# Small parameter loads moved to GpSimd's queue, eight unread products, and two changes of order in an attention and mLSTM trunk

## The chip, the cores and the metric

One core of a Trainium2 chip runs the whole program. The metric is device microseconds of one execution, from a batch of runs that gives a median. A profiled execution of the same program gives the spans, waits and clocks below.

## What is computed

A trunk of two layers over 256 tokens of width 1024, batch 1, in float32. Layer 0 mixes tokens by native sparse attention (16 heads in 4 groups, a compressed, a selected and a sliding branch), layer 1 by a chunkwise mLSTM. Each layer is modulated by a conditioning vector c:

```
shift, scale, gate = split(c @ ada_w[i] + ada_b[i], 3)
h = rmsnorm(x, norm_g[i]) * (1 + scale) + shift
y = nsa_mixer(h, ...) if i == 0 else mlstm_mixer(h, ...)
x = x + gate * y
...
return rmsnorm(x, final_g)
```

In the attention, `k_cmp` and `v_cmp` come from a small two-layer network over blocks of tokens (weights `a_cmp_w1`, `a_cmp_w2`, biases `a_cmp_b1`, `a_cmp_b2`, positions `a_cmp_pe`). The mLSTM has a short convolution on q and k (`b_conv_w`, `b_conv_b`) and a gain per column (`b_head_g`).

## The kernel before, in words

Weights stream from HBM as float32 into a ring of ten raw tiles. Each is split in two fp32r halves, high (`wh`, ScalarE, L165) and low (`wl`, VectorE, L170), and a float32 product is made of three fp32r products on TensorE. The order of the work in layer 0 is written out by hand: inside `manual_schedule` (L387) the instructions of TensorE, ScalarE, VectorE and SyncE stand as the program lists them. GpSimd is not in that list, so a scheduler places its instructions.

**First phase** (`first_phase`, L392, some 60 us). The input projection runs over eight blocks of 128 rows of the weight. For block kk the products are `proj` (L470 to L480): 42 of 128x256 at L480, in three groups of wh, wl and the low half of the activations. Before a block can start, its 128 columns of shift and scale must be known. They come from 1 MB of `ada_w` for each block (tiles `Q`, `KH`, `KL`, multiplied by c on ScalarE at L423 and VectorE at L425 into `adaA`), and `columns` (L427) sums them over partitions by eight products with a single column (L432), after which VectorE adds biases (L434, L435) and ScalarE makes the block's activations (L439). `columns` for block kk + 1 stands after product 30 of block kk, and for the first block after its last product, so that TensorE has nothing to do until L439 is done.

**SyncE's queue** issues every big load, in the order of use (`_load_one`, L72 to L92). Of one block these are 512 KB and 384 KB of `a_w_in` and four of 256 KB of `ada_w`. The fourteen small parameter loads of `small_loads` (L325; 428 KB together) stand in a list, and from the thirteenth big load on one of them follows each big load (L89, L90):

```
for dst, src in pieces:
    self.nc.sync.dma_start(dst(v), src)
if self.small and self.loaded >= self.SMALL:
    self.nc.sync.dma_start(*self.small.pop(0))
```

Five fill `pra` (positions, gains and biases of layer 0 and 1), three fill `prb` (the mLSTM's convolution and gains), and six are the compression network's biases and second weights (`b1bc`, `b2v`, `w2k`, `w2v`). `parameters` (L460), in the seventh block, turns `pra` and `prb` by two TensorE transpositions into columns.

**Attention** (`nsa`, L581). Eight more blocks project the remaining keys and values (`kv_block`), then the compression network (`hidden`, L606, two halves around the scores `S(0)`), then the scores `S(n)`, the exponentials `softmax(n)` (ScalarE, L988), their scaling `scaled(n, j)` (VectorE, L1005), transpositions `T_pair` (L1018) and values `PV` (L1039), for n from 0 to 7, with parts of the z path and of the gates between them. `z_out` (L918) reads the PSUM bank of the z path, and `gate_steps` (L922) takes the same bank over with 16 products at L227. `dup_split` (L559) copies keys between partitions on GpSimd (L571), once at the end of the first phase and once before `S(0)`. GpSimd otherwise makes masks and zeroes tiles.

Of the kernel before, what the change touches and what calls it, by code (L numbers as in the profile page):

```python
# [12 lines left out]
OP = mybir.AluOpType  # L13
AX = mybir.AxisListType

P = 128
# [7 lines left out]
class Kernel:  # L24
# [14 lines left out]


    RAW = 10
    SMALL = 12
    WBUF = 6

    def stream_init(self):
# [26 lines left out]
    def _load_one(self):  # L72
        kind, shape, pieces = self.queue[self.loaded]
        n = int(np.prod(shape[1:]))
        if self.loaded in self.homes:
            tag, part, bufs = self.homes[self.loaded]
            if not part:
                self.guests[tag] = self.T(self.p1, [P, 2048] if bufs == 1 else [P, 1024], tag=tag, bufs=bufs)
            raw = self.guests[tag][:, 1024 * part :]
        else:  # L80
            raw = self.pw.tile([P, 1024], F32, name=self.nm("raw"), tag="raw", bufs=self.RAW)
        v = raw[:, :n]
        if len(shape) == 3:
            v = v.rearrange("p (a b) -> p a b", a=shape[1])
        elif len(shape) == 4:
            v = v.rearrange("p (a b c) -> p a b c", a=shape[1], b=shape[2])
        for dst, src in pieces:
            self.nc.sync.dma_start(dst(v), src)  # L88
        if self.small and self.loaded >= self.SMALL:  # L89
            self.nc.sync.dma_start(*self.small.pop(0))  # L90
        self.raws[self.loaded] = v
        self.loaded += 1  # L92

# [231 lines left out]
    def small_loads(self):  # L325
        nc, t = self.nc, self.t
        row = lambda ap: ap.rearrange("(a p) -> a p", p=P)
        self.small = []
        self.small.append((self.pra[0:32], t["a_cmp_pe"][0].rearrange("j (u r) d -> (j u) (r d)", r=2)))
        self.small.append((self.pra[32:40], row(t["norm_g"][1])))  # L330
        self.small.append((self.pra[40:56], row(t["ada_b"][1, 0:2048])))
        for j in range(2):
            self.small.append((self.pra[56:57, 64 * j : 64 * j + 64], t["a_cmp_b2"][0, 0:1]))
        self.small.append((self.prb[0:64], t["b_conv_w"][0].rearrange("j (c p) -> (j c) p", p=P)))
        self.small.append((self.prb[64:80], row(t["b_conv_b"][0])))
        self.small.append((self.prb[80:96], row(t["b_head_g"][0])))
        for j in range(2):
            self.small.append((self.b1bc[64 * j : 64 * j + 64], t["a_cmp_b1"][0, j].partition_broadcast(64)))
        self.small.append((self.b2v, t["a_cmp_b2"][0, 1].partition_broadcast(P)))
        for j in range(2):  # L340
            self.small.append((self.w2k[:, :, j], t["a_cmp_w2"][0, 0].rearrange("(a p) d -> p a d", p=P)))
        self.small.append((self.w2v, t["a_cmp_w2"][0, 1].rearrange("(a p) d -> p a d", p=P)))


    def layer1(self):
        nc, t, pc, p1 = self.nc, self.t, self.pc, self.p1
        ident = self.ident
# [36 lines left out]
        self.stream_rest()  # L384
        self.small_loads()

        with self.tc.manual_schedule(engines={mybir.EngineType.PE, mybir.EngineType.Activation, mybir.EngineType.DVE, mybir.EngineType.SP}):  # L387
            self.first_phase(place)
            self.nsa(self.acc)
            self.boundary()  # L390

    def first_phase(self, place):  # L392
# [3 lines left out]
        bt = self.bank(6)  # L396
# [30 lines left out]
        def columns(kk, A):  # L427

            bank = self.bank(7)
            for b in range(2):  # L430
                for h in range(2):
                    nc.tensor.matmul(bank[:, b : b + 1], A[:, h, b * P : b * P + P], self.ones1, start=(h == 0), stop=(h == 1), skip_group_check=True)  # L432
            cols = self.T(pc, [P, 2], tag="cols", bufs=4)
            nc.vector.tensor_tensor(cols, bank[:, 0:2], pca[:, 16 + kk : 25 + kk : 8], op=OP.add)  # L434
            nc.vector.tensor_tensor(cols[:, 1:2], cols[:, 1:2], pca[:, 8 + kk : 9 + kk], op=OP.mult)  # L435
            return cols

# [22 lines left out]
        def parameters():  # L460
            bt = self.bank(7)
            nc.tensor.transpose(bt[:, 0:57], self.pra, ident[:57, :57])
            nc.tensor.transpose(bt[:, 64:160], self.prb, ident[:96, :96])
            nc.vector.tensor_copy(pca[:, 32:89], bt[:, 0:57])
            nc.vector.tensor_scalar(pca[:, 80:88], pca[:, 80:88], 1.0, None, op0=OP.add)
            pcb = self.pcb = self.T(pc, [P, 96])
            nc.vector.tensor_copy(pcb[:, 0:80], bt[:, 64:144])
            nc.vector.tensor_scalar(pcb[:, 80:96], bt[:, 144:160], 0.5, None, op0=OP.mult)

        def proj(kk):  # L470

# [34 lines left out]
        for kk in range(KC):  # L506

            if not kk:
                self.make_lo(*wide)
            if kk < KC - 1:  # L510
                A = self.T(pc, [P, 512], tag="adaA", bufs=2).rearrange("p (h m) -> p h m", h=2)
                rows(A, 0)
            if kk:
                h32 = self.T(p1, [P, SEQ], tag="y32", bufs=2)
                modulate(kk, h32, cols)
                rest(kk, h32)
            if kk < KC - 1:
                rows(A, 1)
            if kk:
                self.make(place[kk][1])  # L520
            if kk < KC - 1:
                parts = self.make_hi(place[kk + 1][0])
            else:
                self.mpos = max(place[kk]) + 1
                self.split_next()
            for n, _ in enumerate(proj(kk)):
                if (kk, n) == (6, 34):
                    parameters()
                if kk < KC - 1 and n == (29 if kk else 41):
                    cols = columns(kk + 1, A)  # L530
                    modulate(kk + 1, self.hh[:, kk + 1], cols)
                    self.make_lo(*parts)
                elif (kk, n) == (KC - 1, 17):
                    self.KH, self.KL = [self.T(p1, [P, 4, 512], F32R, tag=tag) for tag in ("KH", "KL")]
                    self.dup_split((self.KH, self.KL), 0, acc[6])
                    self.E, self.F = [], {}
                    self.evac_cmp(acc[4])
                    self.split_next()
                    self.evac_cmp(acc[5])
# [41 lines left out]
    def nsa(self, acc):  # L581
# [62 lines left out]
        self.S(0)  # L644
        self.softmax(0)
        hidden(2)
        hidden(3)

        h1 = self.T(p1, [P, 256], tag="y32", bufs=2)
# [105 lines left out]
        for a in range(2):  # L755
            nc.gpsimd.memset(Pc[a], 0.0)
            nc.vector.tensor_tensor(Pc[a][:, :, 0:16], Tc[:, a], mn[:, 16 * a : 16 * a + 16].unsqueeze(2).to_broadcast([P, 16, 16]), op=OP.mult)
        self.go(z, 8)
        self.S(3)
        self.scaled(2, 0)  # L760
        PcT = self.PcT = self.T(p1, [P, 4, SEQ])

        def cmp_transposed(i2):
# [4 lines left out]
            nc.scalar.activation(PcT[:, 2 * i2 : 2 * i2 + 2].rearrange("p i k -> p (i k)"), b, AF.Copy)  # L768

        cmp_transposed(0)  # L770
        self.softmax(3, (0,))
        self.scaled(2, 1)
        self.z_tanh(1)
        self.z_out(1)
        self.PV(1)
        self.gated(0, 0)

# [937 lines left out]
```

## Time and profile before

| What | us |
|---|---|
| median of 3 runs (459.8 to 460.69) | 460.62 |
| the profiled execution | 459.5 |
| its span, first to last instruction | 457.7 |
| TensorE busy in the span | 441.4 |
| VectorE, ScalarE, GpSimd busy | 340.7, 278.0, 37.9 |

The profiled execution is 1.1 us under the median. The page cuts the span in 40 slices of 11.4 us; digits are tenths of busy time, and PEclk is TensorE's granted clock in tenths of full speed. The chain of waits runs back from the last instruction to what released each step. An "x8" behind a row says that eight instructions are merged in it, so the start of the next row tells the pace.

### The profile page before, as it was taken

To read this page: it belongs to the slowest core of one execution; us is meant where nothing else is said; L and a number is where in the kernel's file an instruction comes from. 1 tells how busy PE (TensorE), PEld (TensorE's weight loads), DVE (VectorE), ACT (ScalarE), POOL (GpSimd) and SP (SyncE) were. 2 spreads that over 40 slices of the span, in tenths; PEclk is the share of its full clock that TensorE was granted. 3 is DMA by queue.
4 is the path that set the end of the run, shared out by engine and by line. 5 is a ranking of instruction groups with operands and counts; after the bars stand their busy time and mean duration, and the time that the engine had idled before them with its cause. 6 is when DMAs were issued, how large, how long until landed. Compare 5 with 4: busy or idle time off the path is not lost.

```text
span 457.7 us, 8171 instructions
## 1 busy us (share of the span) xinstructions
PE 441.4 (96%) x2938; PEld 378.5 (83%) x2938; DVE 340.7 (74%) x792; ACT 278.0 (61%) x549; POOL 37.9 (8%) x102
## 2 busy tenths in 40 slices
PE   7899899999999999999999999999999999999993
PEld 3899899889948777788899889988888888888882
DVE  3878768778959767587998369688986978545645
ACT  4746678466688588366956685655655555454614
POOL 8840020300000000012000000000000000000000
PEclk9989999999999999999999999999999999999997
DMA  8999996793377999899999999897845799740002
GB/s 271 337 313 297 338 373 188 200 364 91 95 208 253 275 236 307 254 194 164 215 172 115 95 291 314 155 170 232 261 127 204 203 230 243 245 139 0 1 0 93
DMA packets 74637, 94.58 MB, mean 207 GB/s; under 512 B 4652, under 2 KB 52068, under 8 KB 74596
## 3 DMA queue, kind: packets, MB, share of 16 engines
q1 hardware_dynamic: 74020, 92.73, 76.2%
q10 hardware_dynamic: 336, 0.80, 0.5%
q8 instruction: 23, 0.38, 0.3%
q0 software_dynamic: 240, 0.53, 0.3%
q14 instruction: 18, 0.15, 0.1%
HBM read 93.00 MB, written 1.05 MB: 205 GB/s over the span
## 4 chain that ended last, share of the span: by engine, by line
PE 82%; DMA 6%; DVE 5%; ACT 3%; SPq 2%; issue 1%; ACTq 0%
PE bank L579 9%; PE bank L577 9%; PE bank L578 9%; PE bank L1162 8%; PE bank L1673 5%; PE bank L1671 5%; PE bank L873 5%; PE bank L1672 5%; PE bank L480 5%; PE bank L1276 4%; DMA raw<-in_a_w_in 3%; PE bank L227 2%; PE bank L1039 2%; PE bank L1509 2%; PE bank L1018 2%; SPq L88 2%
## 5 line engine op out<-in xcount | busy, mean ns | idle before, releaser
L170 DVE TENSOR_TENSOR wl<-raw,wh 128x1024 fp32r<-128x1024 f32 (+4 forms) x127 | 140.2, 1117 | 47.5 <-ACT wh L165 46.3
L165 ACT ACTIVATE wh<-raw 128x1024 fp32r<-128x1024 f32 (+4 forms) x127 | 120.7, 970 | 71.8 <-PE bank L579 27.5
L577 PE MATMUL bank<-wh,one 128*128 128x512 f32 (+1 forms) x208 | 76.8, 370 | 0.7 <-ACT tz L551 0.7
L578 PE MATMUL bank<-wl,one 128*128 128x512 f32 (+1 forms) x208 | 76.3, 367 | 0.0
L579 PE MATMUL bank<-wh,one 128*128 128x512 f32 (+1 forms) x208 | 76.3, 368 | 0.0
L1673 PE MATMUL bank<-one,wl 128*128 128x256 f32 x208 | 59.5, 286 | 0.5 <-DVE wl L170 0.5
L1671 PE MATMUL bank<-one,wh 128*128 128x256 f32 x208 | 59.6, 286 | 0.0
L1672 PE MATMUL bank<-one,wh 128*128 128x256 f32 x208 | 59.0, 284 | 0.0
L577 PEld LDWEIGHTS bank<-wh,one 128*128 128x128 f32 x208 | 39.2, 189 | 6.7 <-ACT tz L551 0.9
L579 PEld LDWEIGHTS bank<-wh,one 128*128 128x128 f32 x208 | 39.2, 188 | 6.1
L578 PEld LDWEIGHTS bank<-wl,one 128*128 128x128 f32 x208 | 39.2, 189 | 5.9
L1673 PEld LDWEIGHTS bank<-one,wl 128*128 128x128 f32 x208 | 39.8, 191 | 1.1 <-DVE wl L170 0.7
L1671 PEld LDWEIGHTS bank<-one,wh 128*128 128x128 f32 x208 | 39.8, 191 | 0.7 <-ACT Pr L988 0.4
L1672 PEld LDWEIGHTS bank<-one,wh 128*128 128x128 f32 x208 | 39.8, 191 | 0.1
L480 PE MATMUL bank<-one,wh 128*128 128x256 f32 x224 | 32.9, 294 | 3.1 <-ACT wh L165 1.7
L480 PEld LDWEIGHTS bank<-one,wh 128*128 128x128 f32 x224 | 29.6, 199 | 3.9 <-ACT wh L165 2.1
L988 ACT ACTIVATE Pr<-Pr,mn 128x128 f32<-128x128 f32 (+1 forms) x64 | 28.2, 444 | 3.6 <-DVE mn L976 3.6
L1162 PE MATMUL bank<-wl,QK 128*128 128x512 f32 (+1 forms) x80 | 28.2, 353 | 0.0
L1162 PE MATMUL bank<-wh,V 128*128 128x512 f32 (+1 forms) x80 | 28.0, 350 | 0.1
L1162 PE MATMUL bank<-wh,QK 128*128 128x512 f32 (+1 forms) x80 | 28.0, 350 | 0.0
L1490 DVE SCALAR_TENSOR_TENSOR conv<-bank,one,conv 128x255 f32<-128x255 f32 (+2 forms) x48 | 20.2, 470 | 2.1 <-ACT conv L1485 2.1
L976 DVE CUSTOM_DVE_ANT_0 Pr<-bank,one 128x128 f32<-128x128 f32 (+1 forms) x64 | 18.4, 352 | 4.2 <-PE bank L962 4.2
(331 smaller groups left out, 786.9 us busy)
## 6 DMA issues: line engine op xcount, KB each, us to landing
raw<-in_b_w_in SPq DMA_DIRECT2D x62, 512.0 KB, 8.6
raw<-in_ada_w SPq DMA_DIRECT2D x34, 512.0 KB, 6.2
raw<-in_b_w_out SPq DMA_DIRECT2D x16, 512.0 KB, 7.2
raw<-in_a_w_in SPq DMA_DIRECT2D x8, 512.0 KB, 6.9
Q<-in_ada_w SPq DMA_DIRECT2D x16, 256.0 KB, 6.3
raw<-in_a_cmp_w SPq DMA_DIRECT2D x8, 512.0 KB, 4.0
raw<-in_a_w_in SPq DMA_DIRECT2D x16, 256.0 KB, 4.2
raw<-in_a_w_out SPq DMA_DIRECT2D x16, 256.0 KB, 6.5
```

What stands on the lines that cost most here:

```text
L165: self.nc.scalar.activation(v(hi), src, AF.Copy)
L170: self.nc.vector.tensor_sub(v(lo), src, v(hi).bitcast(F32))
L480: nc.tensor.matmul(out, w[:, ch * P : ch * P + P], h[:, kk], start=(kk == 0 and m == 0 and ch % 2 == 0), stop=(kk == 7 and m == 2), skip_g ...
L577: nc.tensor.matmul(out, self.hh[:, kk, sl], wh, start=first, stop=False, skip_group_check=True)
L578: nc.tensor.matmul(out, self.hh[:, kk, sl], wl, start=False, stop=False, skip_group_check=True)
L579: nc.tensor.matmul(out, self.hl[:, kk, sl], wh, start=False, stop=last, skip_group_check=True)
L873: nc.tensor.matmul(out, l[:, sl], w[:, c0:c1], start=(k == 0 and m == 0), stop=(k == 7 and m == 2), skip_group_check=True)
L988: self.nc.scalar.activation(v, v, AF.Exp, bias=mn[:, a, br, j : j + 1], scale=-1.0, accum_out=sm[:, a, br, j : j + 1])
L1162: ins = nc.tensor.matmul(out, l[:, sl], w[:, c0:c1], start=(k == 0 and m == 0), stop=(k == N - 1 and m == 2), skip_group_check=True)
L1671: nc.tensor.matmul(out, wh, self.hh[:, kk], start=first, stop=False, skip_group_check=skip)
L1672: nc.tensor.matmul(out, wh, self.hl[:, kk], start=False, stop=False, skip_group_check=skip)
L1673: nc.tensor.matmul(out, wl, self.hh[:, kk], start=False, stop=last, skip_group_check=skip)
```

## The change

- `small_loads` issues the five loads of `pra` at once on GpSimd's queue. The other nine are issued on that queue in the eighth block, behind the first `dup_split`. SyncE's queue has big loads alone. GpSimd joins the engines in written order.
- The transposition of `prb` and the two VectorE instructions that read it move from `parameters` to a place between the compression network's third and fourth quarter.
- In `columns` for the second block, eight products of 128x256 are added that write columns 256 to 511 of the same bank; nothing reads them.
- `scaled(2, 0)` stands before `S(3)`; `z_tanh(1)` and `z_out(1)` stand before `softmax(3, (0,))` and `scaled(2, 1)`.

```
-        if self.small and self.loaded >= self.SMALL:
-            self.nc.sync.dma_start(*self.small.pop(0))
...
         for j in range(2):
             self.small.append((self.pra[56:57, 64 * j : 64 * j + 64], t["a_cmp_b2"][0, 0:1]))
+        for dst, src in self.small:
+            nc.gpsimd.dma_start(dst, src)
+        self.small = []
         self.small.append((self.prb[0:64], t["b_conv_w"][0].rearrange("j (c p) -> (j c) p", p=P)))
...
-        with self.tc.manual_schedule(engines={mybir.EngineType.PE, mybir.EngineType.Activation, mybir.EngineType.DVE, mybir.EngineType.SP}):
+        with self.tc.manual_schedule(engines={mybir.EngineType.PE, mybir.EngineType.Activation, mybir.EngineType.DVE, mybir.EngineType.Pool, mybir.EngineType.SP}):
...
             nc.vector.tensor_tensor(cols, bank[:, 0:2], pca[:, 16 + kk : 25 + kk : 8], op=OP.add)
+            for n in range(8 if kk == 1 else 0):
+
+                nc.tensor.matmul(bank[:, 256:512], self.hh[:, 0, 0:P], self.hh[:, 0], start=True, stop=True, skip_group_check=True)
...
                     self.dup_split((self.KH, self.KL), 0, acc[6])
+                    for dst, src in self.small:
+                        nc.gpsimd.dma_start(dst, src)
...
         self.go(z, 8)
+        self.scaled(2, 0)
         self.S(3)
-        self.scaled(2, 0)
...
         cmp_transposed(0)
+        self.z_tanh(1)
+        self.z_out(1)
         self.softmax(3, (0,))
         self.scaled(2, 1)
-        self.z_tanh(1)
-        self.z_out(1)
```

How the instructions move is shown at three places. In these lists the names in brackets are the semaphores that an instruction waits for: an engine's, or DMAHW0 to 7 and DMASW0 to 7 for loads of the hardware and software queues.

TensorE after the last product of the first block, in the changed program: `columns` for the second block, the added products, and the second block's start.

```order
L432 MATMUL bank_422<-one_14_90,adaA_340 128x1 [waits DVE_49,Activation_49]
L432 MATMUL bank_422<-one_14_90,adaA_340 128x1 [waits DVE_49]
L432 MATMUL bank_422<-one_14_90,adaA_340 128x1 x2
L437 MATMUL bank_422<-one_4_68 128x256 [waits DVE_49]
L437 MATMUL bank_422<-one_4_68 128x256 x7
L479 MATMUL bank_332<-one_4_68,wh_370 128x256 [waits Activation_49]
```

The products at L437 are new. They wait for VectorE's reading of the bank that they share with `columns`, and stand ahead of the product that waits for ScalarE's L439.

SyncE's queue for the sixth and seventh block, before:

```order
L90 DMA one_18_93<-in_b_head_g 16x128 [waits DMAHW0_49]
L88 DMA Q_366<-in_ada_w 128x4x128 [waits DMAHW1_49,DVE_49]
L88 DMA Q_366<-in_ada_w 128x4x128 [waits DMAHW2_49]
L90 DMA one_24_105<-in_a_cmp_b 64x256 [waits DMAHW3_49]
L88 DMA Q_377<-in_ada_w 128x4x128 [waits DMAHW4_49,DVE_49]
L88 DMA Q_377<-in_ada_w 128x4x128 [waits DMAHW5_49]
L90 DMA one_24_105<-in_a_cmp_b 64x256 [waits DMAHW6_49]
L88 DMA raw_381<-in_a_w_in 128x1024 [waits DMAHW7_49]
L90 DMA one_26_106<-in_a_cmp_b 128x64 [waits DMAHW0_49]
L88 DMA raw_384<-in_a_w_in 128x768 [waits DMAHW1_49]
```

and GpSimd's in the eighth block, with the change:

```order
L572 CAST KL_941<-KL_941 64x2x256 [waits DVE_49]
L536 DMA one_18_93<-in_b_conv_w 64x128
L536 DMA one_18_93<-in_b_conv_b 16x128 [waits DMASW0_49]
L536 DMA one_18_93<-in_b_head_g 16x128 [waits DMASW1_49]
L536 DMA one_24_105<-in_a_cmp_b 64x256 [waits DMASW2_49]
L536 DMA one_24_105<-in_a_cmp_b 64x256 [waits DMASW3_49]
L536 DMA one_26_106<-in_a_cmp_b 128x64 [waits DMASW4_49]
L536 DMA one_28_107<-in_a_cmp_w 128x2x64 [waits DMASW5_49]
L536 DMA one_28_107<-in_a_cmp_w 128x2x64 [waits DMASW6_49]
L536 DMA one_30_108<-in_a_cmp_w 128x2x64 [waits DMASW7_49]
L572 CAST KH_940<-KH_940 64x2x256 [waits Activation_49] x2
```

On SyncE every load waits for the landing of the one eight places ahead of it, small or big. With the change the L90 rows are gone from there, and nine of them stand on GpSimd between the first and the second `dup_split`, on eight semaphores of their own.

VectorE in the attention, from the end of `S(3)` on, before (`Pr_1525` and `Pr_1526` are the two halves of `scaled(2)`, L920 is `z_out(1)`):

```order
L976 ISA Pr_1712,mn_1709<-bank_1700,one_38_116 128x256
L976 ISA mn_1709 128x1
L1005 TENSOR_SCALAR Pr_1525<-Pr_1525,f_1660 128x128
L1005 TENSOR_SCALAR Pr_1525<-Pr_1525,f_1660 128x256
...
L1005 TENSOR_SCALAR Pr_1526<-Pr_1526,f_1660 128x128
L1005 TENSOR_SCALAR Pr_1526<-Pr_1526,f_1660 128x256
L920 SCALAR_TENSOR_TENSOR xT_1329<-zb_1740,bank_1622 128x2x256
L1049 TENSOR_TENSOR y_333_1753<-bank_1570,xT_1329 128x512
```

and with the change:

```order
L983 ISA Pr_1725,mn_1722<-bank_1713,one_38_116 128x256
L983 ISA mn_1722 128x1
L927 SCALAR_TENSOR_TENSOR xT_1338<-zb_1741,bank_1631 128x2x256
L1012 TENSOR_SCALAR Pr_1535<-Pr_1535,f_1669 128x128
L1012 TENSOR_SCALAR Pr_1535<-Pr_1535,f_1669 128x256
...
L1056 TENSOR_TENSOR y_334_1762<-bank_1579,xT_1338 128x512
```

`z_out(1)` now stands directly behind the score reductions; four of the eight scalings went ahead of them and four behind it.

## Rows read from the trace of the kernel before

**Rows 1.** The page: TensorE's busy time and share, then the granted clock and the DMA engines' busy share in 40 slices of the span.

```profile
PE 441.4 (96%) x2938; PEld 378.5 (83%) x2938; DVE 340.7 (74%) x792; ACT 278.0 (61%) x549; POOL 37.9 (8%) x102
...
PEclk9989999999999999999999999999999999999997
DMA  8999996793377999899999999897845799740002
```

**Rows 2.** Busy time by stretch around the start of the second block. Columns: the stretch and its length, busy us of TensorE, its weight loads, VectorE, ScalarE and GpSimd with instruction counts, the granted clock, the DMA share, GB/s.

```profile
19.70:20.85 1.15, 0.01 (x2) 0.00 (x1) 1.07 (x3) 0.66 (x2) 1.02 (x3) 1.00 1.19 318
...
22.30:25.70 3.40, 3.40 (x19) 3.40 (x18) 2.79 (x6) 1.58 (x2) 3.09 (x7) 0.50 1.15 316
25.70:45.00 19.30, 19.30 (x164) 19.25 (x164) 15.84 (x34) 10.84 (x18) 3.01 (x7) 1.00 1.07 307
```

**Rows 3.** TensorE in order of time over the first phase: start, us, line, shapes, count, and in brackets idle time before with what ended it. L432 is `columns`, L480 the block's products; each L480 row is the first after a `columns` or a wait.

```profile
18.57 1.14 PE L432 MATMUL bank<-one,adaA 128*128 128x1 f32 x8
20.85 1.22 PE L480 MATMUL bank<-one,wh 128*128 128x256 f32 x8 [1.14 <-ACT one L439]
...
26.04 0.95 PE L432 MATMUL bank<-one,adaA 128*128 128x1 f32 x8
...
32.12 0.95 PE L432 MATMUL bank<-one,adaA 128*128 128x1 f32 x8
...
38.03 0.95 PE L432 MATMUL bank<-one,adaA 128*128 128x1 f32 x8
...
40.34 1.12 PE L480 MATMUL bank<-one,wh 128*128 128x256 f32 x8
...
43.94 0.95 PE L432 MATMUL bank<-one,adaA 128*128 128x1 f32 x8
...
49.29 1.94 PE L480 MATMUL bank<-one,wh 128*128 128x256 f32 x14 [0.95 <-ACT wh L165]
51.07 0.95 PE L432 MATMUL bank<-one,adaA 128*128 128x1 f32 x8
...
56.23 1.94 PE L480 MATMUL bank<-one,wh 128*128 128x256 f32 x14 [0.77 <-ACT wh L165]
58.01 0.95 PE L432 MATMUL bank<-one,adaA 128*128 128x1 f32 x8
```

**Rows 4.** ScalarE in order of time: its reads of the last `ada_w` tiles (L423) and what they waited for, and, in the attention, `z_tanh(1)` (L916).

```profile
47.10 0.91 ACT L423 ACTIVATE adaA<-Q,one 128x256 f32<-128x256 f32 x2 [1.19 <-DMA Q<-in_ada_w]
...
52.44 0.60 ACT L439 ACTIVATE one<-xT,cols 128x256 fp32r<-128x256 f32 x1 [0.59 <-DVE cols L435]
54.04 0.91 ACT L423 ACTIVATE adaA<-KH,one 128x256 f32<-128x256 f32 x2 [1.00 <-DMA KH<-in_ada_w]
...
124.51 0.58 ACT L916 ACTIVATE zb<-bank 128x512 f32<-128x512 f32 x1
```

**Rows 5.** The small loads on SyncE's queue (line L90): issue times in ns, min/median/max, first and last start; then how long they took to land.

```profile
L90 SPq DMA_DIRECT2D one<-in_a_cmp_b x5: 238/430/1064, 26.6 to 38.0; - x5
L90 SPq DMA_DIRECT2D one<-in_a_cmp_w x3: 379/652/737, 39.3 to 44.8; - x3
...
DMA to landing us min/median/max: 4.3/5.4/6.4
```

**Rows 6.** Busy time by stretch, columns as in Rows 2: two of the small loads are issued in the first stretch, twelve in the others.

```profile
11.50:24.70 13.20, 11.78 (x85) 11.19 (x86) 11.53 (x26) 9.22 (x15) 11.87 (x28) 0.91 1.14 333
24.70:35.60 10.90, 10.90 (x89) 10.85 (x89) 8.26 (x18) 5.72 (x12) 3.95 (x9) 0.95 1.08 312
35.60:43.70 8.10, 8.10 (x70) 8.10 (x69) 7.40 (x17) 4.16 (x7) 0.00 (x0) 1.00 1.07 298
43.70:53.60 9.90, 8.95 (x76) 8.74 (x75) 7.28 (x15) 5.45 (x8) 0.53 (x1) 1.00 1.12 310
```

**Rows 7.** The chain of waits, the step that ends at 53.6: start, us, what.

```profile
47.06 6.56 DMA KH<-in_ada_w
```

**Rows 8.** VectorE in order of time: L434 of the second block's `columns`; the first instruction after the compression network; the eight scalings and `z_out(1)` (L920).

```profile
19.75 0.16 DVE L434 TENSOR_TENSOR cols<-bank,one 128x2 f32<-128x2 f32 x1 [0.92 <-PE bank L432]
...
95.25 0.42 DVE L650 TENSOR_TENSOR y<-bank,one 128x256 f32<-128x256 f32 x1 [2.21 <-PE bank L610]
...
123.71 1.92 DVE L1005 TENSOR_SCALAR Pr<-Pr,f 128x128 f32<-128x128 f32 x8
125.55 0.68 DVE L920 SCALAR_TENSOR_TENSOR xT<-zb,bank 128x512 f32<-128x512 f32 x1
```

**Rows 9.** GpSimd in order of time: the end of the first `dup_split` and the second one; and, from its costliest groups, a load that it issues at 214.4 us (busy us, mean ns, idle before).

```profile
65.23 1.28 POOL L571 CAST KL<-KL 64x512 fp32r<-64x512 f32 x2
...
85.94 1.28 POOL L571 CAST KH<-KH 64x512 fp32r<-64x512 f32 x2
87.27 1.28 POOL L571 CAST KL<-KL 64x512 fp32r<-64x512 f32 x2
...
L1639 POOL DMA_DIRECT2D one<-in_ada_b x1 | 0.6, 619 | 0.3 <-POOL one L1638 0.3
```

**Rows 10.** TensorE in the attention: the start of `S(0)`; the last transpositions before the gate's products, and those (L227).

```profile
89.91 0.39 PE L962 MATMUL bank<-KH,Q 128*128 128x256 f32 x1
...
125.44 0.60 PE L767 MATMUL bank<-one,adaA 128*128 128x128 f32 x4
126.28 1.93 PE L227 MATMUL bank<-raw,one 128*32 128x512 f32 x16 [0.24 <-DVE xT L920]
```

More of the change, by code (lines that the diff above doesn't have):

```diff
@@ L41 @@
     RAW = 10
-    SMALL = 12
     WBUF = 6
@@ L462, in parameters @@
             nc.tensor.transpose(bt[:, 0:57], self.pra, ident[:57, :57])
-            nc.tensor.transpose(bt[:, 64:160], self.prb, ident[:96, :96])
             nc.vector.tensor_copy(pca[:, 32:89], bt[:, 0:57])
             nc.vector.tensor_scalar(pca[:, 80:88], pca[:, 80:88], 1.0, None, op0=OP.add)
-            pcb = self.pcb = self.T(pc, [P, 96])
-            nc.vector.tensor_copy(pcb[:, 0:80], bt[:, 64:144])
-            nc.vector.tensor_scalar(pcb[:, 80:96], bt[:, 144:160], 0.5, None, op0=OP.mult)
         def proj(kk):
@@ L646, in nsa @@
         hidden(2)
+        bt = self.bank(7)
+        nc.tensor.transpose(bt[:, 0:96], self.prb, ident[:96, :96])
+        pcb = self.pcb = self.T(pc, [P, 96])
+        nc.vector.tensor_copy(pcb[:, 0:80], bt[:, 0:80])
+        nc.vector.tensor_scalar(pcb[:, 80:96], bt[:, 80:96], 0.5, None, op0=OP.mult)
         hidden(3)
```

## The prediction, as it was made before the changed kernel ran

> **What bounds the kernel now.** I read the page first. TensorE is busy 96% of the span, its clock dips in one early slice, and the DMA engines are at eight tenths or more in the first six slices and often again in the middle [rows 1]. So the time is TensorE's own work, and only what makes TensorE idle or slow can be won. The view by stretches shows the dip: in the second block the granted clock is 0.50 for 3.40 us, that is 1.2 instead of 2.4 GHz, right after a stretch of 1.15 us in which TensorE did nothing [rows 2]. TensorE's own order of time gives the pace: `columns` returns every 5.91 us (32.12, 38.03, 43.94) where nothing disturbs it, then after 7.13 and 6.94 us [rows 3]. In these two long blocks TensorE waits for ScalarE, and ScalarE had waited 1.19 and 1.00 us for `ada_w` tiles [rows 4]. Last, the queue view and the rates: small loads take as long to land as big ones, 5.4 us in the middle [rows 5], and the stream runs at 333 GB/s before most of them and at 298 to 312 among them [rows 6].
>
> **The eight products.** TensorE idles from 19.71 to 20.85 because the second block's activations wait for VectorE and ScalarE. The order shows that the new products wait for VectorE's read of their bank, which ends at 19.91 [rows 8]. At full clock a 128x256 product takes 0.12 us (30 of them from 40.34 to 43.94 [rows 3]), so eight fill 0.96 us and end near 20.9, some 0.1 us after ScalarE would have let the block start. That 0.1 us is their cost: one bank, no reader, nothing else behind them. If the clock then stays up, the 30 products of this block, 5.19 us from 20.85 to 26.04, take the 3.60 us of the sixth block's 30 [rows 3]. Gain 1.59 - 0.1 = **1.5 us**. From below it is -0.1 (clock falls anyway), from above 1.7 (the 6.08 us of the next block are another 0.17 over 5.91). I take 1.5: what stood before the fall was 1.15 us without work behind products of one column, and the later waits of 0.95 and 0.77 us, with full products around them, brought no fall [rows 1, 3].
>
> **The small loads leave SyncE's queue.** Every load there waits for the landing of the eighth before it, so a load of 4 KB holds a place as long as one of 512 KB. The two long blocks lost 7.13 - 5.91 and 6.94 - 5.91, together **2.25 us** [rows 3], and that is all that this part can give. Does the stream get early enough? The read of the first two `KH` tiles was due at about 53.0 (end of L439) and they landed at 53.6 [rows 4, 7]. With TensorE 1.5 us ahead and the first stall of 1.22 gone it is due at 50.3. From 24.7 to that landing the stream carries four blocks of 1,920 KB and 512 KB, 8.39 MB; at 333 GB/s [rows 6] that is 25.2 us, landing at 49.9: early by 0.4. The stretch of 333 has slightly less of `ada_w` in it (48% of the bytes, not 53%), which comes in rows of 512 bytes where `a_w_in` has 3 and 4 KB, so I take 0.25 us off for caution. Bounds: from below only the small loads' own bytes, 0.44 MB at 333 GB/s or 1.3 us of the stream; from above their places, 14 x 5.4 / 8 = 9.5 us, which is more than TensorE can use. Together with the clock the first phase gives 1.5 + 2.25 - 0.25 = **3.5 us** (from below 1.3, because then the stream sets the pace and eats the clock's gain; from above 3.75).
>
> **Where the loads go.** Five loads in GpSimd's setup cost some 0.6 us each; a load that GpSimd issued at 214.4 took 0.62 us [rows 9]. Their first reader is `parameters` at about 60, and the masks behind them are wanted from 89.9 on [rows 10]. The nine others stand behind the first `dup_split`, which ends at 66.5, and ahead of the second, at 85.94 [rows 9]: 9 x 0.62 = 5.6 us in 19.4 us of idle GpSimd. Cost nothing. The cover is gone if they hold GpSimd over 20.8 us (the second copy may end 1.36 us later than 88.55 before `S(0)` at 89.91 is late), 2.3 us each. The Trainium skill ("SBUF — State Buffer", section "A bandwidth-pool intuition that's wrong (but worth ruling out)") warns of this: a GpSimd load needs a port that a VectorE copy can lock, and 0.62 us became 3.1 us there; by that figure nine loads would hold GpSimd some 28 us. The row at 214.4, with VectorE at work around it, shows no such wait.
>
> The moved transposition of `prb` is one TensorE product in either place, and its two VectorE readers fall in VectorE's idle 2.21 us before L650 [rows 8]: nothing. GpSimd's memsets come behind the second copy, ended by about 91.5; the tiles are first touched after 100: nothing.
>
> **The order in attention.** The gate's products (L227) start at 126.28, freed by `z_out(1)` (L920, from 125.55), while TensorE's work before them, four transpositions of 0.11 from 125.44, ends at 125.88 [rows 8, 10]. Four of the eight scalings (half of 1.84 us, 0.92) now come behind `z_out`, so it ends at about 125.3, and `z_tanh`, which stood at 124.51 [rows 4] behind four exponentials, is done earlier still. TensorE itself is late next, at 125.88: gain **0.4 us**, between 0 and 0.9. The second half of the scalings ends at 126.2 as before; its reader comes after L227, near 127.7.
>
> **Sum.** 3.5 + 0.4 = 3.9 us. Behind 66 us TensorE is busy nearly without a break and loads wait for freed buffers, so I let an early gain last to the end. The profiled execution of 459.5 (span 457.7) would be 455.6; it lies 1.1 under the median of 460.62, and from the median the forecast is **456.7 us**.
>
> **The rivals.**
> - *The DMA engines, not the queue, are the limit.* Their share is 1.07 to 1.12 among the small loads and 1.14 before [rows 6], which leaves little to win beyond bytes. Then phase one gives 1.3, in all 1.7: 458.9. Against it: 298 GB/s where four small loads of a few KB to 64 KB stand between. Chance 0.15.
> - *The clock falls anyway*, a little later, because columns of one element and a rest of 0.2 us remain, or because the products are held. Then 2.25 - 0.1 + 0.4 = 2.55: 458.1. Chance 0.12.
> - *The early gain is lost again*: a later load is as late as before and TensorE waits for it in the key blocks up to 86 us. Only 0.4 remains: 460.2, no change. For it speaks that the DMA engines stay full to the sixth slice; against it, six and seven tenths in the next two [rows 1]. Chance 0.06.
> - *Slower: the loads hold GpSimd.* If VectorE keeps GpSimd from writing a load's descriptors, the second `dup_split` is late, and `S(0)` and all behind it with it. It decides from 2.3 us a load. At the landing time of 5.4 us [rows 5] as the longest that one load could hold it, 48.6 - 20.8 = 27.8 us late: 484.5. By the Trainium skill's 3.1 us it would be 7.1 us late, or 463.8. Against it 0.62 us at 214.4 [rows 9]. Chance 0.04.
>
> **How the numbers follow.** The forecast has the rest, 0.63. The range goes up to the first rival with 0.2 for the spread of runs, 459.1, and down to the full 3.75 + 0.17 + 0.4 = 4.3 with the profiled execution's 1.1 taken off, 455.2; it leaves out the two last rivals and a part of the first. Faster by over 0.2% (0.9 us, what a measurement of this kernel can tell): forecast and first two rivals, 0.90. No change 0.06, slower 0.04.
>
> **What would show it.** Right: no stretch of half clock in the second block; `columns` every 5.9 us up to the last, at about 54.5 instead of 58.01; no wait of ScalarE for `KH` or `Q` over 0.4 us; 330 GB/s from 25 to 50 us; nine GpSimd loads of about 0.6 us done by 70; L227 following the transpositions without idle time. Wrong: half clock again, `columns` apart by 6.5 us or more, or GpSimd's second copy starting later than its ScalarE source allows.

## The result, and the profile after

| | median us | range | executions |
|---|---|---|---|
| kernel before, timed beside it | 460.21 | 459.67 to 460.69 | 4 |
| changed kernel | 455.66 | 455.23 to 456.02 | 4 |
| the changed kernel once more (e10) | 455.66 | 455.56 to 455.68 | 4 |

The ratio is 0.9901, 95% interval 0.9884 to 0.9918: faster by 4.55 us. The forecast was 456.7, range 455.2 to 459.1. The profiled execution took 455.82 (span 454.0, against 457.7), and that of e10 455.56 (span 453.8).

The page of the changed kernel, same lines as in [rows 1]:

```profile
PE 440.7 (97%) x2946; PEld 377.8 (83%) x2946; DVE 342.2 (75%) x792; ACT 278.4 (61%) x549; POOL 46.0 (10%) x116
...
PEclk9999999999999999999999999999999999999997
DMA  8999997792287999898999998897846799740002
```

The dip of the clock is gone. By stretch, columns as in [rows 2, 6]:

```profile
22.30:25.70 3.40, 2.86 (x25) 2.65 (x24) 3.39 (x8) 2.50 (x4) 2.96 (x8) 1.00 1.16 315
...
43.70:53.60 9.90, 9.90 (x85) 9.90 (x86) 8.49 (x19) 6.46 (x12) 0.00 (x0) 1.00 1.12 351
...
63.50:69.10 5.60, 4.59 (x35) 4.14 (x33) 3.33 (x5) 5.42 (x11) 5.36 (x10) 1.00 0.93 289
```

The second block has full clock, but TensorE is idle for 0.54 of the 3.40 us; in the late stretch it has no idle time, and the rate is 351 GB/s. The last row is the stretch of GpSimd's loads. TensorE in order of time, which answers to [rows 3, 10] (L437 are the eight products, L479 is the former L480, L650 the moved transposition, L224 the gate's products):

```profile
18.74 1.13 PE L432 MATMUL bank<-one,adaA 128*128 128x1 f32 x8
20.12 1.21 PE L437 MATMUL bank<-one 128*128 128x256 f32 x8 [0.25 <-DVE cols L434]
21.17 1.12 PE L479 MATMUL bank<-one,wh 128*128 128x256 f32 x8
...
23.79 1.93 PE L479 MATMUL bank<-one,wh 128*128 128x256 f32 x14 [0.54 <-ACT wh L162]
25.56 0.95 PE L432 MATMUL bank<-one,adaA 128*128 128x1 f32 x8
...
49.21 0.95 PE L432 MATMUL bank<-one,adaA 128*128 128x1 f32 x8
55.15 0.95 PE L432 MATMUL bank<-one,adaA 128*128 128x1 f32 x8
...
87.00 0.39 PE L969 MATMUL bank<-KH,Q 128*128 128x256 f32 x1
...
88.58 1.95 PE L611 MATMUL bank<-raw,PT 128*64 128x256 f32 x16
90.46 0.30 PE L650 MATMUL bank<-one,one 96*128 96x96 f32 x1
90.70 1.95 PE L611 MATMUL bank<-raw,PT 128*64 128x256 f32 x16
92.58 0.38 PE L1678 MATMUL bank<-one,wh 128*128 128x256 f32 x1
...
122.93 0.60 PE L774 MATMUL bank<-one,adaA 128*128 128x128 f32 x4
123.46 1.92 PE L224 MATMUL bank<-raw,one 128*32 128x512 f32 x16
```

The long blocks are gone (the last is 5.94 us, from 49.21 to 55.15, before 6.94). `S(0)` starts 2.91 us earlier. The moved transposition stands between two bursts of 16 products, and the gate's products follow their transpositions without idle time. ScalarE, as in [rows 4]: the wait in the second block comes from a late `Q` tile, for which ScalarE waited 0.64 us (the prediction allowed 0.4), and the read of `KH` has no wait:

```profile
21.60 0.91 ACT L423 ACTIVATE adaA<-Q,one 128x256 f32<-128x256 f32 x2 [0.64 <-DMA Q<-in_ada_w]
...
51.18 0.91 ACT L423 ACTIVATE adaA<-KH,one 128x256 f32<-128x256 f32 x2
```

GpSimd, as in [rows 9]:

```profile
63.54 0.57 POOL L536 DMA_DIRECT2D one<-in_b_conv_w  x1
64.11 0.52 POOL L536 DMA_DIRECT2D one<-in_b_conv_b  x1
64.62 0.49 POOL L536 DMA_DIRECT2D one<-in_b_head_g  x1
65.10 1.60 POOL L536 DMA_DIRECT2D one<-in_a_cmp_b  x3
66.69 1.46 POOL L536 DMA_DIRECT2D one<-in_a_cmp_w  x2
68.34 0.72 POOL L536 DMA_DIRECT2D one<-in_a_cmp_w  x1 [0.20 <-issue]
82.61 1.27 POOL L572 CAST KH<-KH 64x512 fp32r<-64x512 f32 x2 [13.55 <-ACT KH L567]
```

The nine loads are issued by 69.06, and the second copy then waits 13.55 us, for ScalarE.

Where the 3.7 us lie is found by lining up the same instructions in both traces and writing down by how much the distance from mark to mark shrank. The second column is e10, the same program again.

| stretch | before | gain, first profile | gain, e10 | forecast |
|---|---|---|---|---|
| to the first columns | 18.57 | -0.17 | 0.07 | 0 |
| first to second columns | 7.47 | 0.65 | 1.39 | 1.5 |
| second to last columns | 31.97 | 2.38 | 1.71 | 2.0 |
| last columns to S(0) | 31.90 | 0.05 | 0.06 | 0 |
| S(0) to the product after L610 | 5.19 | -0.39 | -0.38 | 0 |
| from there to the gate's products | 31.18 | 0.30 | 0.29 | 0.4 |
| from there to the last issue of a load or write | 326.79 | -0.03 | -0.05 | 0 |
| last issue to the end of the span | 4.63 | 0.91 | 0.81 | 0 |
| sum | 457.7 | 3.7 | 3.9 | 3.9 |

### The profile page after: what moved, and what is told of

Same layout as the page of the kernel before. It is cut to its first block, busy times and chain, and to the rows that moved or that the text cites. A ratio compares the mean times of both kernels' runs of the same rounds, so it can differ in the third digit from the quotient of the medians.

```text
span 454.0 us, 8203 instructions
## 1 busy us (share of the span) xinstructions
PE 440.7 (97%) x2946; PEld 377.8 (83%) x2946; DVE 342.2 (75%) x792; ACT 278.4 (61%) x549; POOL 46.0 (10%) x116
## 4 chain that ended last, share of the span: by engine, by line
PE 87%; DMA 3%; SPq 3%; ACT 3%; DVE 3%; issue 1%
PE bank L580 9%; PE bank L578 9%; PE bank L579 9%; PE bank L1169 8%; PE bank L479 6%; PE bank L1680 6%; PE bank L1678 5%; PE bank L1679 5%; PE bank L880 5%; PE bank L1283 4%; SPq L87 2%; PE bank L1046 2%; PE bank L1025 2%; PE bank L224 2%; PE bank L1516 2%; DMA Q<-in_ada_w 2%
## 5 line engine op out<-in xcount | busy, mean ns | idle before, releaser
L1678 PEld LDWEIGHTS bank<-one,wh 128*128 128x128 f32 x208 | 39.8, 191 | 0.7 <-issue 0.4
L1679 PEld LDWEIGHTS bank<-one,wh 128*128 128x128 f32 x208 | 39.8, 191 | 0.2
L479 PE MATMUL bank<-one,wh 128*128 128x256 f32 x224 | 31.5, 286 | 0.8 <-ACT wh L162 0.5
L479 PEld LDWEIGHTS bank<-one,wh 128*128 128x128 f32 x224 | 28.4, 191 | 1.3 <-ACT wh L162 0.7
```

Of the source, the lines that this page charges most:

```text
L479: nc.tensor.matmul(out, w[:, ch * P : ch * P + P], h[:, kk], start=(kk == 0 and m == 0 and ch % 2 == 0), stop=(kk == 7 and m == 2), skip_g ...
L1678: nc.tensor.matmul(out, wh, self.hh[:, kk], start=first, stop=False, skip_group_check=skip)
L1679: nc.tensor.matmul(out, wh, self.hl[:, kk], start=False, stop=False, skip_group_check=skip)
```

## The experiments

The ratio of each is to the kernel before, timed on the same chip with it.

**e1, the products alone.** The kernel before with this:

```
+            for n in range(8 if kk == 1 else 0):
+                nc.tensor.matmul(bank[:, 256:512], self.hh[:, 0, 0:P], self.hh[:, 0], start=True, stop=True, skip_group_check=True)
```

> The kernel before with the eight unread products alone. In the changed kernel the second block ran at full clock, but its columns came only 0.48 us earlier, because the block began 0.3 us later and then waited 0.54 us for a Q tile. Theory: the clock is held by the products alone, so the 30 products of the second block take 3.6 us and a wait for data instead of 5.19 us, columns at 24.7 to 25.6 instead of 26.04; the two long blocks stay long, because the small loads still hold places in SyncE's queue and the stream's landings set them, so the last columns stay at 58.0 within 0.4 and the time at 459.8 to 460.2, no change. Rival (the sum of the prediction): the 1.5 us last to the end, 458.7. Second rival: the clock falls all the same, and the loads' move had been what kept it: columns at 26.1 or later, time 460.2 to 460.4.

460.74 us, ratio 1.0009 (0.9987 to 1.0031): no change. The second block had full clock and 5.89 us from columns to columns, but the clock had fallen earlier, behind another wait; TensorE was idle for 2.01 us just before 8.91:

```profile
8.90:12.20 3.30, 3.29 (x22) 1.51 (x22) 1.73 (x5) 1.78 (x3) 2.95 (x8) 0.51 1.07 363
...
22.30:25.70 3.40, 3.40 (x31) 3.40 (x30) 3.39 (x8) 3.21 (x6) 3.08 (x7) 1.00 1.15 317
```

The theory holds for the last columns (58.38) and for the time as a ratio; that the clock could fall in front of the products was in no expectation. It means that this profile does not show what the products alone are worth: the block was 1.58 us shorter than before, but the earlier fall had made its first columns 1.92 us later.

**e2, the loads alone.** The changed kernel without the products and with attention in the old order.

> The changed kernel without the eight products and with attention in the old order: the moved loads alone (with the moved transposition of prb). Theory: the second block runs at half clock as before (3.40 us at 0.50, 30 products in some 5.2 us), so its columns come at 26.0 to 26.2; from there every 5.9 us without a long block, last columns at 55.7 to 55.9 (2.2 us earlier than 58.01) against 55.15 in the changed kernel; time 456.7 to 457.9. Rival: the prediction's sizes, products 1.5 and loads 2.0 us: last columns at 56.5, time 457.5 to 458.5. Second rival: without the products the stream's slack is larger and the clock's loss is hidden, so that it equals the changed kernel: 455.7.

456.77 us, ratio 0.9913 (0.9885 to 0.9941). There was half clock in the second block as before, then 5.91 us per block to the last columns at 55.54:

```profile
21.80:24.80 3.00, 3.00 (x16) 3.00 (x16) 2.95 (x7) 2.00 (x3) 2.62 (x8) 0.50 1.12 340
```

The theory holds; its range was 456.7 to 457.9. Most of the gain comes with the loads.

**e3, the order alone.** The kernel before with `scaled(2, 0)` ahead of `S(3)`, and `z_tanh(1)`, `z_out(1)` ahead of `softmax(3, (0,))`.

> The kernel before with the two changes of order in attention alone. Theory: the gate's products (L227) follow the four transpositions without idle time; the step shows as a gain of 0.3 us at 126 us that lasts, time 459.9, not told from no change by the times alone. Rival: the scalings ahead of z_out delay another reader and the gain is lost by 140 us: no gain at the marks behind 140. The first 120 us are the same program as before, so the marks there also show how much two profiled executions of one program differ (the last write took 3.65 us to land before and 2.72 after).

459.84 us, ratio 0.9982 (0.9958 to 1.0005), not told from no change. In its trace L227 starts at 125.70, right behind the transpositions from 125.17, and the distance from `S(0)` to there is 36.06 us, before 36.37 [rows 10]: 0.31 us, which lasts.

**e4, all loads early.** The changed kernel with all fourteen on GpSimd's queue in its setup:

```
         self.small.append((self.w2v, t["a_cmp_w2"][0, 1].rearrange("(a p) d -> p a d", p=P)))
+        for dst, src in self.small:
+            nc.gpsimd.dma_start(dst, src)
...
-                    for dst, src in self.small:
-                        nc.gpsimd.dma_start(dst, src)
```

> The changed kernel with all fourteen small loads in GpSimd's setup instead of nine of them in the eighth block: the nine now issue from about 30.5 us on, while the stream is at work. Theory: what was lost before was the places in SyncE's queue, and off that queue the loads cost the stream only their bytes, some 0.42 MB or 1.3 us at 333 GB/s; the KH tiles landed 0.7 us before their reader in the changed kernel, so some 0.5 us show: no stretch between columns over 6.5 us, 455.9 to 456.3. Rival: the loads themselves slow the transfers, on whatever queue (298 to 312 GB/s among them against 333, over 29 us a loss of 2.2 us): a block of 6.5 us or more, time 457 or more. Second rival: nothing, 455.7, as the DMA engines have room.

457.55 us (457.36 to 457.84), ratio 0.9928 (0.99 to 0.9955): 1.9 us more than the changed kernel, which was not timed beside it. The theory falls, the first rival stands. The long blocks are back, although no small load is on SyncE's queue (here L431 is `columns`):

```profile
24.53 0.95 PE L431 MATMUL bank<-one,adaA 128*128 128x1 f32 x8
...
36.74 0.94 PE L431 MATMUL bank<-one,adaA 128*128 128x1 f32 x8
43.50 0.94 PE L431 MATMUL bank<-one,adaA 128*128 128x1 f32 x8
50.38 0.94 PE L431 MATMUL bank<-one,adaA 128*128 128x1 f32 x8
57.15 0.95 PE L431 MATMUL bank<-one,adaA 128*128 128x1 f32 x8
```

From the second to the last columns it took 32.62 us, before 31.97. The queue view from 30.5 to 44 us shows the load on the engines (packets, MB, their time as a share of 16 engines; q1 is SyncE's queue, q0 GpSimd's):

```profile
q1 hardware_dynamic: 4522, 3.80, 98.9%
q0 software_dynamic: 384, 0.42, 12.4%
```

0.124 of 13.5 us is 1.7 us of all sixteen engines, taken from a stream that has no idle engine there.

But the places in SyncE's queue were not free either. Three profiles with the eight products differ in where the small loads stand: all early on SyncE (e1), all early on GpSimd (e4), nine of them late on GpSimd (e10). Their stretch from 24 to 52 us, in this order, ends with the DMA share and GB/s:

```profile
24.00:52.00 28.00, 27.65 (x233) 27.44 (x233) 24.20 (x53) 16.16 (x26) 3.94 (x8) 1.00 1.08 308
...
24.00:52.00 28.00, 26.62 (x221) 26.00 (x221) 23.03 (x49) 16.36 (x26) 13.42 (x24) 1.00 1.13 321
...
24.00:52.00 28.00, 27.98 (x236) 27.68 (x235) 24.57 (x51) 17.79 (x29) 7.61 (x15) 1.00 1.13 333
```

In that stretch SyncE's queue waited 4.7 us for landings in e1, and its list of waits has none in e4 and e10. The last columns came at 58.38, 57.15 and 54.84. So of the 3.5 us between the first and the last, about 1.2 go with the queue and 2.3 with the time of the loads. These are single profiles, and e1 had its early fall of the clock. The times agree that the queue counts: e4 took 457.55 us where e1, timed beside it, took 460.74, though order and end are also in that difference.

**e5, the nine loads late, but on SyncE.** In the changed kernel's eighth block `nc.sync.dma_start` in place of `nc.gpsimd.dma_start`.

> The changed kernel with the nine later small loads on SyncE's queue again, but still in the eighth block, where it has them on GpSimd's. Theory: what cost the time was their place in the first 55 us, where the stream has no room, not the queue as such; behind 60 us the DMA engines are at six and seven tenths, so the first phase stays as in the changed kernel (last columns at 55.2) and the whole at 455.5 to 456.3. Rival (the queue): nine loads of 5.4 us with eight at a time hold the stream of the key blocks by some 6 us, TensorE waits for in_a_cmp_w tiles between 65 and 87 us, and S(0) comes 1 us or more later than 87.00: 456.7 to 460. Beside it: does the last write of the output take 2.7 or 3.65 us to land, with nine transfers more on SyncE than in the changed kernel.

455.68 us, ratio 0.9896 (0.9865 to 0.9927), as the changed kernel. The last columns come at 54.66, `S(0)` at 86.53. The theory holds: behind 60 us the loads cost nothing on SyncE's queue either. It does not show that the queue costs nothing in the first phase. At the end of the kernel no code was fetched (more on this under e6); the landing of the write on ScalarE's queue is not recorded, and the span ends 4.04 us after the last issue.

**e7, loads and products, old order.** The changed kernel without the two changes of order.

> The changed kernel with attention in the old order: moved loads and the eight products. Against the moved loads alone (456.77) it shows what the products are worth, against the changed kernel (455.66) what the order is worth. Theory: the order is 0.3 us, read at 126 us, so 455.95; the products hold the clock in most executions and give 0.5 to 1.4 us in the second block, of which what lies beyond the stream's lead is lost again in waits for tiles: last columns at 54.6 to 55.2, granted clock 0.995 or more in all runs. Rival: without the order the products' gain is lost and it equals the moved loads alone, 456.8. Second rival: the clock falls in other places, as in the kernel with the products alone, where it fell from 8.8 to 12.3 us: clock below 0.994 in several runs and a spread of 2 us or more.

455.90 us (455.65 to 455.98), ratio 0.9898 (0.9867 to 0.9929). The second block took 6.08 us, the last columns came at 54.63, and the granted clock was 0.994 to 0.998. The theory holds, but for a clock of 0.994 in two of five executions, where it said 0.995 or more. Beside e2 (456.5 to 457.67) the products are worth 0.9 us by the medians and 0.7 by the ratios; the two were not timed side by side, and the intervals of the ratios overlap.

**e8 and e11, four and two products.** `range(4 if kk == 1 else 0)` and `range(2 if kk == 1 else 0)`.

> The changed kernel with four unread products instead of eight: they fill 0.5 us of the 1.15 us in which TensorE has nothing to do, and end 0.5 us earlier. Theory: the fall of the clock hangs on how much TensorE is at work there; with half of it the clock falls in some executions (0.50 for some 3 us) and stays in others, so 455.7 to 456.8 with a larger spread than the changed kernel's 0.8 us. Rival: four are enough and save the 0.1 to 0.15 us by which eight were late: 455.5, clock 0.995 or more in all runs. Second rival: four do nothing, half clock as without them, 456.5.

> The changed kernel with two unread products instead of eight (four gave 455.36 us with the clock at 0.995 to 0.998 in five runs; none 456.77, beside 0.3 us of order, with 0.991 to 0.994). Theory: two leave nearly 0.9 us of the gap without work, so the clock falls in most executions as without products: 0.994 or less, 456.2 to 456.5. Rival: any product behind those of one column is enough: 455.4, 0.995 or more in all runs, and no half clock in the second block.

Four: 455.36 us (455.19 to 455.71), ratio 0.9888 (0.9857 to 0.992). Two: 455.95 us (455.81 to 456.17), ratio 0.9897 (0.9845 to 0.9949), mean clock 0.992 to 0.998. Neither profile has half clock in the second block, and both took 6.08 us from columns to columns. For four, the first rival stands. For two, both were off: the clock stayed in the profile, against the theory, but the time is 0.5 us above the rival's 455.4. It is also 0.3 us above that of eight products timed beside it (e10), and those ranges do not overlap; in the profile with two products one later block took 6.66 us (36.66 to 43.32), behind a late `Q` tile. Whether four beat eight (455.66) isn't shown, since the ranges overlap. Nor does one profile show that two or four products hold the clock, as e6 and e12 show next.

**e6, e9 and e12, the code fetch.** In the profile before, a fetch of instructions (queue q14) runs beside the last writes of the output, and in the changed kernel's there is none. The kernel before with two or eight more loads on SyncE's queue, or five on GpSimd's, at about 215 us:

```
+        for n in range(2):
+            spare = self.T(p2, [1, 64])
+            nc.sync.dma_start(spare, t["final_g"][64 * n : 64 * n + 64].unsqueeze(0))
```

> The kernel before with two more loads of 256 bytes on SyncE's queue in the second layer, which nobody reads. In the three profiled kernels that have the small loads on SyncE (before, products alone, order alone) a code fetch of 8 KB runs among the last two writes of the output, at 455 us, and the write on ScalarE's queue takes 3.65 us to land; in the three that have moved them there is no fetch there and it takes 2.72. Theory: the fetch is of SyncE's instructions, and two loads more put it some instructions earlier: no fetch in the last 4 us, 2.7 us to land, 0.9 us off the end, 459.8 beside 460.7. Rival: the fetch is another engine's, or the slow landing has to do with the number of transfers alone: the fetch at 455 and 3.65 us stay, and the time is as before.

> The kernel before with eight instead of two more loads of 256 bytes on SyncE's queue in the second layer (issued at about 215 us). With two the code fetch stayed at 457.9, 1.6 us behind the last issue, and the last write took 3.66 us. Theory: the fetch is of SyncE's instructions, and two loads were too small a shift; eight put the fetch ahead of the last writes (or into the wait of some 40 us before them): no fetch in the last 5 us, 2.7 us to land. Rival: it is not SyncE's code: the fetch stays 1.5 to 2 us behind the last issue and the write takes 3.65 us again. The time itself may be up to 1 us longer, since eight loads hold places in the second layer; the end is read from the last issue on.

> The kernel before with five more loads of 256 bytes on GpSimd's queue at about 215 us, where GpSimd has nothing else to do, unread. With two and with eight more on SyncE's queue the code fetch stayed 1.6 to 2 us behind the last issue and the write took as long as before. The kernel with nine loads back on SyncE and five on GpSimd had no fetch at the end. Theory: the fetch is of GpSimd's instructions, which the changed kernel lengthens by the loads: with five more of them no fetch in the last 5 us, 2.7 us for the last write, 3.8 us from the last issue to the end of the span instead of 4.6 to 4.8. Rival: neither queue's instructions: the fetch is there again 1.5 to 2 us behind the last issue, with 4.6 to 4.8 us to the end, and its origin stays open.

Ratios 1.0008 (0.9988 to 1.0027), 1.0005 (0.9971 to 1.004) and 1.0007 (0.998 to 1.0034). In all three the fetch of 8 KB came again, about 2 us behind the last issue, and the span ended 4.78, 4.70 and 4.61 us after it. All three theories fall. The queue view from 453 us to the end in e12:

```profile
q10 hardware_dynamic: 144, 0.26, 12.8%
q1 hardware_dynamic: 144, 0.26, 12.5%
q14 instruction: 1, 0.01, 0.3%
...
out<-DT ACTq DMA_DIRECT2D x1, 256.0 KB, 3.6
```

and from 449 us to the end in e10:

```profile
q10 hardware_dynamic: 144, 0.26, 14.6%
q1 hardware_dynamic: 144, 0.26, 14.5%
...
out<-DT ACTq DMA_DIRECT2D x1, 256.0 KB, 2.7
```

The six profiles with the loads in the old place have the q14 row, and 3.6 to 3.7 us to land in the five where the landing is recorded; the eight with moved loads have no such row, and 2.7 us in the seven where it is recorded. That the fetch delays the write is argued from this alone; whose code it is stays open. e6 and e12 also showed a second thing: their second block kept full clock without products (6.08 and 6.28 us), and the clock fell in a long wait for tiles instead. The rows are from e6, the first of TensorE in order of time:

```profile
20.81 1.21 PE L480 MATMUL bank<-one,wh 128*128 128x256 f32 x8 [1.14 <-ACT one L439]
...
22.30:25.70 3.40, 3.40 (x30) 3.33 (x29) 2.85 (x7) 1.54 (x2) 3.09 (x7) 1.00 1.16 317
51.00:57.40 6.40, 6.40 (x32) 6.40 (x31) 4.24 (x10) 3.13 (x6) 0.52 (x1) 0.50 1.11 341
```

In front of the fall TensorE had waited 2.66 us for ScalarE, behind a late tile. The columns of that block came 9.82 us after the ones before. In front of the second block TensorE waited the same 1.14 us as in the kernel before, behind the same eight products with a single column, and the clock stayed. So that wait alone does not decide whether the clock falls; what else does stays open.

**e10, the changed kernel again.**

> The changed kernel once more, unaltered, for a second profiled execution and to be timed beside two and four products. In its first profile the second block waited 0.54 us for a Q tile and the columns came 0.48 us earlier than before; in the three profiled executions since then with moved loads and products (eight in two, four in one) the second block took 6.08 us from columns to columns, 1.39 less than before. Theory: the wait for the tile was one execution's; now 6.1 us from the first columns to the second, last columns at 54.6 to 54.9, granted clock 0.994 or more in all runs, time 455.7. Rival: the wait belongs to the changed kernel: 6.8 us again, last columns at 55.1 or later.

455.66 us, ratio 0.989 (0.9838 to 0.9941). The theory holds:

```profile
18.50 1.14 PE L432 MATMUL bank<-one,adaA 128*128 128x1 f32 x8
19.89 1.21 PE L437 MATMUL bank<-one 128*128 128x256 f32 x8 [0.25 <-DVE cols L434]
20.94 1.12 PE L479 MATMUL bank<-one,wh 128*128 128x256 f32 x8
...
24.58 0.95 PE L432 MATMUL bank<-one,adaA 128*128 128x1 f32 x8
...
54.84 0.95 PE L432 MATMUL bank<-one,adaA 128*128 128x1 f32 x8
```

6.08 us from columns to columns; the wait for `Q` was the first execution's own.

## Why the prediction was right, and where its steps were not

The time fell into the range, near its lower end, but not only for the reasons given: two terms were off, and one gain was not in the sum at all.

- **The eight products, 1.5 us.** Right in size for the block: 1.39 in e10, 0.65 in the first profile, where the late `Q` tile took 0.54 back. As an edit by itself they gave nothing (e1). In each of the six profiles with the loads in the old place the clock falls once: at the second block in three (before, e3, e9), at 8.8 us in e1, at 50 us in e6 and e12. In the seven with moved loads and products it doesn't fall while TensorE is at work. In the second block itself it fell in four of six profiles without unread products (before, e2, e3, e9) and in none of eight with them, which says that they hold it there. That they are worth their sum only once the other waits are gone is argued from e1, e6 and e12.
- **The small loads, 2.25 less 0.25 us.** Right in size (2.38 and 1.71), but the cause named was the smaller part. The step "a load of 4 KB holds a place as long as one of 512 KB" put all on the places in the queue. e4 freed them and kept the long blocks; its last columns came 1.2 us earlier than those of e1. Another 2.3 us came when nine of the fourteen loads left the first phase, for 63.5 us. So the rival that the DMA engines are the limit named the larger part, 12.4% of all engines' time for 0.42 MB. It was too small, however: it gave the first phase 1.3 us, the bytes of the loads, and the first phase gained 2.9 and 3.2, with the clock's gain in it.
- **How far the stream leads.** `KH` had no recorded wait at 51.18. The two gains trade with each other, as the lower bound said: where the second block is short (e10), the later blocks have small waits and give 1.71; where it is long (first profile, e2), they all run at 5.91.
- **GpSimd's loads, nothing.** Right: 0.49 to 0.73 us each, with VectorE busy for 3.33 of the 5.60 us from 63.5 to 69.1. The wait of 3.1 us that the Trainium skill ("SBUF — State Buffer", section "A bandwidth-pool intuition that's wrong (but worth ruling out)") reports for such a load is not in this trace. But that figure is for a load under a VectorE copy, and VectorE ran TENSOR_TENSOR and SCALAR_TENSOR_TENSOR here, so the trace does not test it. Nor did the row at 214.4 that the prediction held against it: VectorE was idle from 214.14 to 215.31, through all of that load.
- **The moved transposition, nothing.** Wrong: 0.4 us. The two VectorE readers cost nothing, but TensorE paid for the product itself: the next burst starts 0.24 us later, and the whole from `S(0)` on takes 5.58 us against 5.19 (5.57 or 5.58 in all eight profiles with the moved transposition). In its old place it had cost 0.06 at most, if the stretch to `S(0)` gained by nothing else.
- **The order, 0.4 us.** 0.30; L224 follows at the pace of TensorE, as forecast, 0.53 us behind the start of the four transpositions rather than the 0.44 that was assumed.
- **Not in the sum: the end.** 0.8 to 0.9 us, which made up for the transposition and for the rest of the first phase. Without it the profiled gain would have been 2.8 to 3.1 us, and the sum of 3.9 too large. That the sum met the profiles so well is luck.
- **From the profile to the median.** The sum was taken off the median of 460.62, and the measured median lies 1.0 us lower than that gives. One execution did not stand for the kernel before: its 66 executions timed beside the experiments went from 458.7 to 464.8 us. The eight with a mean granted clock of 0.988 or less had a median of 462.7, the ten with 0.994 or more 459.5. The changed kernel's eight had 0.994 to 0.998 and 455.2 to 456.0. This suggests that the change also takes away falls of the clock that the profiled execution did not have, such as the one of e6. The narrow spread does not need late loads: e4's six executions, with the nine loads early on GpSimd's queue, lie within 0.5 us.

## What to carry to other kernels

When small loads delay a stream, ask first whether the DMA engines have idle time there. Where they have none, another queue gives back only what the places in the first one cost (here some 1.2 us), and the larger part (2.3 us) comes from moving the loads to a time with room. A fall of the clock is not tied to one place; remove the long waits before filling one of them. Read the spread of many executions and their mean clocks before taking one profile's stall for the typical one.

## What the runs showed of the hardware

After the same wait of 1.14 us behind the same products the granted clock fell to half in four of six profiles and stayed in two; with two to eight unread products in that gap it stayed in all eight. Nine small loads of 0.42 MB took 12.4% of all sixteen DMA engines for 13.5 us. A fetch of 8 KB of code beside the last two writes went with 0.9 us more until the write landed (3.6 to 3.7 against 2.7 us), at the same bytes written. And one transposition of 96 columns, put between two bursts of 16 products, cost 0.4 us.
